# Two attention query projections: three 256-column matmuls per block against one of 512 and one of 256 columns

## The chip, the cores and the metric

One core of one Trainium2 chip runs the whole kernel. The metric is the device time in microseconds (us) of one execution; several executions are timed and their median stands for the kernel.

## The reference

The program is two layers of a decoder trunk on 256 tokens of width 1024, in float32. What matters here, cut down:

```python
for l in range(2):
    h  = layer_norm(ALPHA * x + 0.5 * swiglu(x, w_gu1, w_down1))
    dn_q, dn_k, dn_v, ..., sw_q, sw_k, sw_v, xa_q, gates = split(h @ w_in)
    o_dn = gated_deltanet(dn_q, dn_k, dn_v, ...)              # convolution, SiLU, recurrence
    o_sw = sliding_window_attention(sw_q, sw_k, sw_v, sinks)  # 8 query heads of 64
    o_xa = memory_cross_attention(xa_q, mem_n, w_mem_kv)      # 4 query heads of 128
    h = layer_norm(ALPHA * h + merge(gates, o_dn, o_sw, o_xa) @ w_out)
    x = layer_norm(ALPHA * h + 0.5 * swiglu(h, w_gu2, w_down2))
```

The change is about `xa_q` and `sw_q`, the queries of the two attentions: two products of h (256 x 1024) with a 1024 x 512 part of `w_in`.

## The kernel before

**Split operands.** Every float32 operand of a large product is held as two float32r tiles: hi, the rounded value, and lo, what the rounding left. `split` (lines 115 to 117) makes them: a cast on ACT (line 116), then a subtraction on DVE (line 117). A product is the sum of three: hi by hi, hi by lo, lo by hi.

**Weights.** All weights lie in one stream in the order of their use. `unit` (lines 98 to 113) issues on SP the transfer of the next 1024 columns (512 KB) and splits them into `whi` and `wlo`; there are three raw buffers and five of each split kind. The split of a unit has a raised priority, 300 ahead in the planner's order.

**Activations.** The normalised stream lies transposed in `hT`, 8 blocks of 128 channels by 256 tokens. `new_hT` makes one tile of shape 128 x 8 x 2 x 256, so that a block's hi and lo parts lie side by side: hT[0] is hi, hT[1] is lo, and hT[2][:, k] is both, 512 columns.

**Two ways to project.** `projB_parts` (lines 151 to 165) takes for each block k and each 128-wide output tile t three matmuls of 256 columns, whi by hi, whi by lo and wlo by hi, all into the same half of one PSUM bank; two output tiles share a bank. `halves` (lines 187 to 191) does so for a 512-wide output in two halves of two tiles and gives each finished bank to `use`. `shares` (lines 167 to 185) serves the feed-forward layers: for a block it takes one matmul of 512 columns, whi by hi and lo side by side, into a whole bank of the tile, and one of 256 columns, wlo by hi, into the bank's first half. The sum is then made outside: ACT copies the second half to SBUF (line 183) and DVE adds the first half to it (line 184).

**PSUM.** Matmul results of projections go to the pool `psA`, four banks taken in turn: whoever allocates the fifth waits until the first one's readers are done.

**Order.** Inside `mixers` the flag `pinned` keeps PE's instructions in the order of the program text. For the other engines a planner puts instructions in order by priority, at compile time. `weave(work, steps)` (lines 137 to 141) advances a generator and issues other steps after its n-th part; a half has two parts, one for each unit of weights. The stages of `mixers` around the change are, in order: z, gates of DeltaNet and sw_v (648 columns); the halves of DeltaNet's k, q and v, each followed by `conv`'s `use` (ACT line 486 and six DVE instructions of line 489 per half, which read the bank, then SiLU on ACT, line 490), with the transposes `tok_k` and `tok_q` woven in; then

```python
        weave(halves(xt, use_xq), {3: [tok_v]})
        (b,) = projB(xt, 1, 8)
        ...
        weave(halves(xt, use_sq), {
            1: [decay],
            2: [lambda: spread(0), lambda: x_scores(0)],
            3: [lambda: spread(1)],
            4: [lambda: products(0, 0), lambda: products(0, 1)]})
```

Here `use_xq` and `use_sq` split the finished bank into the hi and lo tiles of the queries (the tiles named u and sql in the profile). `projB(xt, 1, 8)` is sw_k, one unit of weights. `tok_v` transposes the finished v (8 matmuls of line 129) and needs v's last SiLU. `decay` is four small matmuls on g, which DVE makes with a chain of small instructions (lines 550 to 574). After the stage comes `gates(0)`, with matmuls of 512 columns and two banks of `psA` at a time.

Of the kernel before, what the change touches and what calls it, by code (L numbers as in the profile page):

```python
# [17 lines left out]
P = 128  # L18
# [20 lines left out]
def tile_trunk(ctx, tc, x, xT, mem, wst, lnp, memln, cvw, rows, cst, out):  # L39
# [14 lines left out]
    def nm(s):  # L54
        uid[0] += 1
        return f"{s}_{uid[0]}"

    def T(pool, shape, tag, dt=F32, bufs=None):
        kw = {} if bufs is None else {"bufs": bufs}
        return pool.tile(shape, dt, tag=tag, name=nm(tag), **kw)  # L60

    def acc():
        return T(psA, [P, 512], "acc")
# [35 lines left out]
    def unit(w=U, dst=None, cuts=1, behind=None):  # L99
        ahead = tc.high_priority(offset=AHEAD) if pos[0] >= 8 * P * U else nullcontext()  # L100
        raw = T(praw, [P, U], "raw")
        src = wst[pos[0]:pos[0] + P * w].rearrange("(p w) -> p w", p=P)
        pos[0] += P * w
        (ph, th), (pl, tl) = dst or ((phi, "whi"), (plo, "wlo"))
        with ahead:
            hi = T(ph, [P, U], th, F32R)
            lo = T(pl, [P, U], tl, F32R)
            for i in range(cuts):
                c = slice(i * w // cuts, (i + 1) * w // cuts)
                nc.sync.dma_start(raw[:, c], src[:, c])  # L110
                with tc.issue_after(behind) if behind else nullcontext():
                    split(hi[:, c], lo[:, c], raw[:, c])
        return hi, lo

    def split(hi, lo, src):
        nc.scalar.copy(hi, src)  # L116
        return nc.vector.tensor_tensor(lo, src, hi.bitcast(F32), op=ALU.subtract).ins  # L117
# [3 lines left out]
    def pe(ins):  # L121

        return tc.keep_in_program_order(ins) if pinned[0] else ins

    def matmul(*a, **k):
        return pe(nc.tensor.matmul(*a, **k))  # L126
# [10 lines left out]
    def weave(work, steps):  # L137

        for n, _ in enumerate(work, 1):
            for f in steps.get(n, ()):  # L140
                f()

    def projB(xt, nt, kpu, behind=None):
        g = projB_parts(xt, nt, kpu, behind)
        while True:
            try:
                next(g)
            except StopIteration as e:
                return e.value

    def projB_parts(xt, nt, kpu, behind=None):
        banks = [acc().rearrange("p (t s) -> p t s", t=2) for _ in range((nt + 1) // 2)]
        for uu in range(KD // kpu):
            hi, lo = unit(behind=behind)
            for kk in range(kpu):
                k = uu * kpu + kk
                for t in range(nt):
                    c = (kk * nt + t) * P
                    o = banks[t // 2][:, t % 2, :]
                    lastt = t % 2 == 1 or t == nt - 1  # L160
                    matmul(o, hi[:, c:c + P], xt[0](k), start=(k == 0 and t % 2 == 0), stop=False, skip_group_check=True)
                    matmul(o, hi[:, c:c + P], xt[1](k), start=False, stop=False, skip_group_check=True)
                    matmul(o, lo[:, c:c + P], xt[0](k), start=False, stop=(k == KD - 1 and lastt), skip_group_check=True)
            yield
        return banks

    def shares(hT, behind=None):


        banks = [acc() for _ in range(2)]  # L170
        for uu in range(2):
            hi, lo = unit(behind=behind)
            for kk in range(4):
                k = uu * 4 + kk
                cs_ = [slice((kk * 2 + t) * P, (kk * 2 + t + 1) * P) for t in range(2)]

                for t in range(2):
                    matmul(banks[t], hi[:, cs_[t]], hT[2][:, k], start=k == 0, stop=False, skip_group_check=True)
                for t in range(2):
                    matmul(banks[t][:, 0:S], lo[:, cs_[t]], hT[0][:, k, :], start=False, stop=k == KD - 1, skip_group_check=True)  # L180
        y = T(p2, [P, 2, S], "t2", bufs=4)
        for t in range(2):
            nc.scalar.copy(y[:, t], banks[t][:, S:])  # L183
            nc.vector.tensor_tensor(y[:, t], y[:, t], banks[t][:, 0:S], op=ALU.add)  # L184
        return y

    def halves(xt, use):

        for i in range(2):
            (b,) = yield from projB_parts(xt, 2, 4)  # L190
            use(i, b)
# [54 lines left out]
    def new_hT():  # L246

        t = T(pu, [P, KD, 2, S], "hT", F32R)
        return t[:, :, 0, :], t[:, :, 1, :], t

    def acc_of(t):
        return (lambda k: t[0][:, k, :], lambda k: t[1][:, k, :])
# [61 lines left out]
    class Ffn:  # L314
# [54 lines left out]
        def rest(self, hT, tail, dsts, post, mid={}, behind=None):  # L369
            for f in range(2, NFT):  # L370
                y = shares(hT, behind if f == 2 else None)
                nc.scalar.activation(y[:, 0], y[:, 0], AF.Silu)  # L372
                hf = y[:, 1]
                nc.vector.tensor_tensor(hf, y[:, 0], hf, op=ALU.mult)  # L374
                t = self.h(f // 2)
                split(t[:, 0, f % 2, :], t[:, 1, f % 2, :], hf)
                if f in mid:
                    mid[f]()
            outs = full_rows()
            projA((lambda k: self.hu[k // 2][:, 0, k % 2, :], lambda k: self.hu[k // 2][:, 1, k % 2, :]), D, 1, NFT, outs, tail, dsts, after=post)  # L380
# [79 lines left out]
    def mixers(l, hT, mkT, mv_, post):  # L460
        xt = acc_of(hT)
# [79 lines left out]
        def col(tag):  # L541
            return T(pu, sh, tag)
# [11 lines left out]
        t = col("spt")  # L554
        nc.vector.tensor_tensor(t, ba[:, :, 4:8], rowb(rw[:, l, 12:16]), op=ALU.add)
        e = col("spe")
# [16 lines left out]
        g = col("g")  # L573
# [182 lines left out]
        def use_sq(i, b):  # L756
            split(*(t[:, 2 * i:2 * i + 2, :] for t in sq_), b)

        weave(halves(xt, use_xq), {3: [tok_v]})
        (b,) = projB(xt, 1, 8)  # L760
        for kv in range(2):
            hs = slice(kv * 64, kv * 64 + 64)
            split(swk[0][hs, kv, :], swk[1][hs, kv, :], b[hs, 0, :])
        weave(halves(xt, use_sq), {
            1: [decay],
            2: [lambda: spread(0), lambda: x_scores(0)],
            3: [lambda: spread(1)],
# [223 lines left out]
    hT = new_hT()  # L991
# [20 lines left out]
    for l in range(NL):  # L1012
        mT = []
        mid = memory_T(mT, l)
        if l == 0:
            mid.update({5: small, 7: lambda: xres(0), 9: lambda: xres(1)})
        post = Post(lnp[l, 0, 0], lnp[l, 0, 1])
        f1.rest(hT, 4, [((pu, "u12"), (pu, "u13")), ((p2, "gt"), (p2, "gt"))], post, mid, ends)
        kv = memory_kv(mT, post.end)
        if l == 0:  # L1020
            nc.scalar.activation(nea, rw[:, :, 8:12], AF.Exp)
            nc.vector.tensor_scalar(nea, nea, -1.0, None, ALU.mult)
        post2 = Post(lnp[l, 1, 0], lnp[l, 1, 1])
        mixers(l, post.hT, *kv, post2)
        f2 = Ffn()
        begin(f2, post2.hT)
        last = l == NL - 1
        post = Post(lnp[l, 2, 0], lnp[l, 2, 1], last)
        f2.rest(post2.hT, 6, [((pu, a), (pu, b)) for a, b in (("w0", "w1"), ("w2", "w3"), ("u11", "u12"))] + [((pu, "u13"), (p2, "pp"))], post, behind=post2.end)
        ends = post.end  # L1030
        if not last:
            f1, hT = Ffn(), post.hT
            begin(f1, hT)
# [86 lines left out]
```

## Time and profile before

| | |
|---|---|
| time, median of 3 runs | 1296.47 us (1295.87 to 1298.31) |
| the profiled execution's own time | 1298.02 us |
| its span, first to last instruction | 1296.2 us |
| PE / weight loads / DVE / ACT / POOL busy | 99% / 86% / 69% / 55% / 6% |
| granted TensorE clock, mean | 0.998 of full speed |

A line of the timeline reads: start (us from the span's start), how long it was busy, engine, line, operation, tiles written <- tiles read, shape, and how many neighbours were merged; in brackets the idle time of the engine ahead of it and what ended it. Ends of matmuls are modelled, so that two matmuls in a row overlap in the record; from start to start is what one costs.

### The profile page before, as it was taken

Reading aid. Unit: us, or ns where it says so; the run is one execution under the profiler, and the core shown is the slowest. Engines: PE = TensorE matmul, PEld = TensorE weight load, DVE = VectorE, ACT = ScalarE, POOL = GpSimd, SP = SyncE. Lnnn points to the kernel's source line nnn. Section 1 sums busy time; section 2 is a strip of 40 time slices with the busy share of each in tenths; the row PEclk is TensorE's granted clock in tenths of the full one; section 3 lists DMA queues with packets and bytes.
Section 4 is the critical chain, followed back from the end, with each engine's and each line's share of the span. In section 5 each row is a group of like instructions: output and inputs, shape, how many; then the busy total and the mean of one; then the engine's idle time right before and its main releaser. Section 6 shows DMA issues by size and latency. Waiting matters only on the chain.

```text
span 1296.2 us, 20444 instructions
## 1 busy us (share of the span) xinstructions
PE 1277.9 (99%) x7832; PEld 1116.2 (86%) x7832; DVE 888.4 (69%) x1430; ACT 708.5 (55%) x1177; POOL 77.2 (6%) x135
## 2 busy tenths in 40 slices
PE   8999999999999999999999999999999999999997
PEld 6888889999878888888888888899988788888886
DVE  6787556796647777665677674759867388777645
ACT  6656444666674546554455654456656654565541
POOL 0000000102311000000000000000033100000000
PEclk9999999999999999999999999999999999999999
DMA  7867564654533636555665555556453256455553
GB/s 266 276 210 244 193 229 128 220 174 135 161 131 130 228 129 211 191 185 192 228 222 200 188 186 192 199 175 201 163 165 131 98 182 224 149 194 194 189 189 111
DMA packets 68577, 240.25 MB, mean 185 GB/s; under 512 B 8160, under 2 KB 9312, under 8 KB 68480
## 3 DMA queue, kind: packets, MB, share of 16 engines
q1 hardware_dynamic: 66176, 232.53, 53.1%
q0 software_dynamic: 2304, 6.43, 1.8%
q8 instruction: 61, 1.00, 0.3%
q14 instruction: 36, 0.29, 0.1%
HBM read 235.64 MB, written 3.28 MB: 184 GB/s over the span
## 4 chain that ended last, share of the span: by engine, by line
PE 89%; DVE 4%; DMA 4%; ACT 2%; issue 1%; SPq 0%; DVEq 0%; ACTq 0%
PE acc L126 78%; PE at L126 4%; DMA raw<-in_wst_dram 3%; PE sm L126 3%; PE sm L129 1%; ACT whi L116 1%; DVE wlo L117 1%; PE acc L340 1%; PE acc L337 1%; DMA pp<-in_mem_dram 1%; PE acc L338 1%; PE at L129 1%; DVE bnst L282 0%; DVE u L117 0%; DVE h L301 0%
## 5 line engine op out<-in xcount | busy, mean ns | idle before, releaser
L117 DVE TENSOR_TENSOR wlo<-raw,whi 128x1024 fp32r<-128x1024 f32 (+2 forms) x403 | 487.4, 1214 | 308.7 <-ACT whi L116 307.2
L116 ACT CAST whi<-raw 128x1024 fp32r<-128x1024 f32 (+2 forms) x403 | 414.4, 1033 | 366.7 <-DMA raw<-in_wst_dram 99.0
L126 PE MATMUL acc<-hT,whi 128*128 128x512 f32 (+1 forms) x1952 | 524.9, 357 | 0.0
L126 PEld LDWEIGHTS acc<-hT,wlo 128*128 128x128 f32 x1616 | 304.6, 189 | 56.0
L126 PE MATMUL acc<-hT,wlo 128*128 128x256 f32 x1616 | 347.6, 279 | 0.0
L126 PEld LDWEIGHTS acc<-hT,whi 128*128 128x128 f32 x1952 | 299.8, 190 | 0.2
L126 PE MATMUL acc<-whi,u 128*128 128x512 f32 (+1 forms) x800 | 246.7, 373 | 0.0
L126 PEld LDWEIGHTS acc<-whi,u 128*128 128x128 f32 x800 | 150.1, 188 | 27.7 <-DVE t L184 1.2
L126 PE MATMUL acc<-whi,hT 128*128 128x512 f32 (+1 forms) x544 | 168.4, 380 | 5.6 <-ACT whi L116 5.6
L126 PE MATMUL acc<-wlo,u 128*128 128x512 f32 (+1 forms) x400 | 148.4, 371 | 0.0
L126 PEld LDWEIGHTS acc<-whi,hT 128*128 128x128 f32 x544 | 100.6, 189 | 23.7 <-ACT whi L116 5.6
L126 PE MATMUL acc<-wlo,hT 128*128 128x512 f32 (+1 forms) x272 | 101.9, 375 | 0.0
L126 PEld LDWEIGHTS acc<-wlo,u 128*128 128x128 f32 x400 | 75.5, 189 | 12.2
L372 ACT ACTIVATE t<-t 128x256 f32<-128x256 f32 x80 | 33.4, 417 | 60.4 <-DVE t L184 59.9
L184 DVE TENSOR_TENSOR t<-t,acc 128x256 f32<-128x256 f32 x160 | 59.9, 415 | 0.0
L126 PEld LDWEIGHTS acc<-wlo,hT 128*128 128x128 f32 x272 | 51.5, 190 | 8.2 <-DVE wlo L117 0.9
L183 ACT COPY t<-acc 128x256 f32<-128x256 f32 x160 | 51.5, 369 | 0.1
L116 ACT CAST u<-t 128x256 fp32r<-128x256 f32 x80 | 32.1, 401 | 20.4 <-DVE t L374 20.4
L374 DVE TENSOR_TENSOR t<-t 128x256 f32<-128x256 f32 x80 | 33.9, 424 | 9.2 <-ACT t L372 7.7
L126 PE MATMUL at<-whi,u 128*128 128x256 f32 x152 | 39.0, 283 | 0.0
L117 DVE TENSOR_TENSOR u<-t,u 128x256 fp32r<-128x256 f32 x80 | 33.6, 420 | 7.1 <-ACT u L116 7.1
L489 DVE SCALAR_TENSOR_TENSOR t<-acc,cw,t 128x255 f32<-128x255 f32 (+2 forms) x72 | 34.5, 479 | 0.9
(248 smaller groups left out, 1250.4 us busy)
## 6 DMA issues: line engine op xcount, KB each, us to landing
raw<-in_wst_dram SPq DMA_DIRECT2D x409, 512.0 KB, 3.6
raw<-in_wst_dram SPq DMA_DIRECT2D x16, 324.0 KB, 3.0
gB<-in_lnp_dram SPq DMA_DIRECT2D x6, 512.0 KB, 6.4
bB<-in_lnp_dram SPq DMA_DIRECT2D x6, 512.0 KB, 5.9
mdr<-w POOLq DMA_DIRECT2D x4, 512.0 KB, 6.8
w<-dr POOLq DMA_DIRECT2D x4, 512.0 KB, 8.8
w<-mdr POOLq DMA_DIRECT2D x4, 512.0 KB, 5.2
t<-in_xT_dram SPq DMA_DIRECT2D x4, 256.0 KB, 5.3
```

Of the source, the lines that this page charges most:

```text
L116: nc.scalar.copy(hi, src)
L117: return nc.vector.tensor_tensor(lo, src, hi.bitcast(F32), op=ALU.subtract).ins
L126: return pe(nc.tensor.matmul(*a, **k))
L129: return pe(nc.tensor.transpose(*a))
L183: nc.scalar.copy(y[:, t], banks[t][:, S:])
L184: nc.vector.tensor_tensor(y[:, t], y[:, t], banks[t][:, 0:S], op=ALU.add)
L337: nc.tensor.matmul(ps, hT[0][:, k, ts], hi[:, c], start=k == 0, stop=False)
L338: nc.tensor.matmul(ps, hT[0][:, k, ts], lo[:, c], start=False, stop=False)
L340: nc.tensor.matmul(ps, hT[1][:, k, ts], hi[:, c], start=False, stop=k == KD - 1)
L372: nc.scalar.activation(y[:, 0], y[:, 0], AF.Silu)
L374: nc.vector.tensor_tensor(hf, y[:, 0], hf, op=ALU.mult)
L489: nc.vector.scalar_tensor_tensor(yc[:, j, d:], b[:, j, :S - d], w[:, t:t + 1], yc[:, j, d:], op0=ALU.mult, op1=ALU.add)
```

## The change

`shares` becomes a generator, `shares_parts`, that yields after each unit of weights and can be woven; the old `shares` runs it to its end, so the feed-forward layers issue what they issued. A new `wide_halves` runs it twice for a 512-wide output, and the queries of both attentions use it in place of `halves`. The split of the queries (`use_xq`, `use_sq`) then reads a sum in SBUF and not a bank.

```diff
     def shares(hT, behind=None):
-
-
-        banks = [acc() for _ in range(2)]
-        for uu in range(2):
+        g = shares_parts(hT, behind)
+        while True:
+            try:
+                next(g)
+            except StopIteration as e:
+                return e.value
+
+    def shares_parts(hT, behind=None, nt=2):
+        kpu = 8 // nt
+        banks = [acc() for _ in range(nt)]
+        for uu in range(nt):
             hi, lo = unit(behind=behind)
-            for kk in range(4):
+            for kk in range(kpu):
...
-                for t in range(2):
+                for t in range(nt):
                     matmul(banks[t], hi[:, cs_[t]], hT[2][:, k], start=k == 0, stop=False, skip_group_check=True)
-                for t in range(2):
+                for t in range(nt):
                     matmul(banks[t][:, 0:S], lo[:, cs_[t]], hT[0][:, k, :], start=False, stop=k == KD - 1, skip_group_check=True)
+            yield
         y = T(p2, [P, 2, S], "t2", bufs=4)
-        for t in range(2):
+        for t in range(nt):
             nc.scalar.copy(y[:, t], banks[t][:, S:])
             nc.vector.tensor_tensor(y[:, t], y[:, t], banks[t][:, 0:S], op=ALU.add)
         return y
+
+    def wide_halves(hT, use):
+
+        for i in range(2):
+            use(i, (yield from shares_parts(hT)))
...
-        weave(halves(xt, use_xq), {3: [tok_v]})
+        weave(wide_halves(hT, use_xq), {3: [tok_v]})
...
-        weave(halves(xt, use_sq), {
+        weave(wide_halves(hT, use_sq), {
```

## Rows read from the trace of the kernel before

**Rows 1.** The page: busy time of the engines, slices, the chain that ended last.

```profile
PE 1277.9 (99%) x7832; PEld 1116.2 (86%) x7832; DVE 888.4 (69%) x1430; ACT 708.5 (55%) x1177; POOL 77.2 (6%) x135
...
PE 89%; DVE 4%; DMA 4%; ACT 2%; issue 1%; SPq 0%; DVEq 0%; ACTq 0%
```

**Rows 2.** By stretch: length, PE, PEld, DVE, ACT, POOL busy, clock, DMA share, GB/s.

```profile
235.00:271.00 36.00, 36.00 (x304) 36.00 (x303) 32.63 (x63) 22.92 (x35) 2.38 (x2) 1.00 0.58 200
271.00:284.00 13.00, 13.00 (x111) 13.00 (x110) 11.69 (x25) 8.25 (x13) 0.00 (x0) 1.00 0.47 160
284.00:304.00 20.00, 20.00 (x170) 19.92 (x169) 14.22 (x32) 12.76 (x26) 3.12 (x2) 1.00 0.47 159
```

**Rows 3.** Timeline of PE, first layer: first half of xa_q, second half's first row.

```profile
271.26 0.40 PE L126 MATMUL acc<-hT,whi 128*128 128x256 f32 x2
271.50 0.28 PE L126 MATMUL acc<-hT,wlo 128*128 128x256 f32 x1
...
277.02 0.40 PE L126 MATMUL acc<-hT,whi 128*128 128x256 f32 x2
```

**Rows 4.** Timeline of PE, feed-forward layer: two passes of the other scheme.

```profile
63.87 0.62 PE L126 MATMUL acc<-hT,whi 128*128 128x512 f32 x2
64.33 0.40 PE L126 MATMUL acc<-hT,wlo 128*128 128x256 f32 x2
...
75.02 0.63 PE L126 MATMUL acc<-hT,whi 128*128 128x512 f32 x2
```

**Rows 5.** Groups by line: weight load, copy and add of the other scheme, split.

```profile
L126 PEld LDWEIGHTS acc<-hT,whi 128*128 128x128 f32 x1952 | 299.8, 190 | 0.2
...
L184 DVE TENSOR_TENSOR t<-t,acc 128x256 f32<-128x256 f32 x160 | 59.9, 415 | 0.0
L183 ACT COPY t<-acc 128x256 f32<-128x256 f32 x160 | 51.5, 369 | 0.1
```

**Rows 6.** Timeline of DVE, first layer: end of v's convolution, split of xa_q.

```profile
276.45 1.51 DVE L489 SCALAR_TENSOR_TENSOR t<-acc,cw,t 128x255 f32<-128x255 f32 x3
278.18 1.23 DVE L117 TENSOR_TENSOR wlo<-raw,whi 128x1024 fp32r<-128x1024 f32 x1 [0.22 <-ACT whi L116]
```

**Rows 7.** Timeline of ACT, first layer: around the end of xa_q's first half.

```profile
274.22 1.05 ACT L116 CAST whi<-raw 128x1024 fp32r<-128x1024 f32 x1 [0.94 <-PE acc L126]
275.17 0.47 ACT L486 ACTIVATE t<-acc,cw 128x256 f32<-128x256 f32 x1
277.10 1.05 ACT L116 CAST whi<-raw 128x1024 fp32r<-128x1024 f32 x1 [1.46 <-PE acc L126]
```

**Rows 8.** From a DVE result to PE's start: timelines of DVE and PE.

```profile
459.63 1.41 DVE L301 SCALAR_TENSOR_TENSOR h<-h,rstd,bB 128x512 f32<-128x512 f32 x2
...
460.53 0.63 PE L129 MATMUL sm<-cs,h 128*128 128x128 f32 x4 [0.97 <-DVE h L301]
```

**Rows 9.** The same place in the second layer: PE, then DVE.

```profile
916.92 0.40 PE L126 MATMUL acc<-hT,whi 128*128 128x256 f32 x2
...
916.35 1.51 DVE L489 SCALAR_TENSOR_TENSOR t<-acc,cw,t 128x255 f32<-128x255 f32 x3
```

**Rows 10.** First layer, PE: tok_v, sw_k's start, sw_q's start.

```profile
279.90 1.04 PE L129 MATMUL sm<-cs,u 128*128 128x128 f32 x8
280.69 0.48 PE L126 MATMUL acc<-hT,whi 128*128 128x256 f32 x2
...
286.52 0.40 PE L126 MATMUL acc<-hT,whi 128*128 128x256 f32 x2
```

**Rows 11.** First layer, ACT then DVE: split of xa_q's second half and its neighbours.

```profile
283.72 1.05 ACT L116 CAST whi<-raw 128x1024 fp32r<-128x1024 f32 x1 [1.98 <-PE acc L126]
...
285.01 1.23 DVE L117 TENSOR_TENSOR wlo<-raw,whi 128x1024 fp32r<-128x1024 f32 x1
...
286.23 0.69 DVE L117 TENSOR_TENSOR u<-acc,u 128x512 fp32r<-128x512 f32 x1
...
287.44 0.17 DVE L574 TENSOR_TENSOR g<-spp,nea 128x8 f32<-128x8 f32 x1
```

More of the change, by code (lines that the diff above doesn't have):

```diff
@@ L167, in shares @@
     def shares(hT, behind=None):
-        banks = [acc() for _ in range(2)]
-        for uu in range(2):
+        g = shares_parts(hT, behind)
[8 more added lines that the diff above has]
+        for uu in range(nt):
             hi, lo = unit(behind=behind)
-            for kk in range(4):
-                k = uu * 4 + kk
-                cs_ = [slice((kk * 2 + t) * P, (kk * 2 + t + 1) * P) for t in range(2)]
-                for t in range(2):
+            for kk in range(kpu):
+                k = uu * kpu + kk
+                cs_ = [slice((kk * nt + t) * P, (kk * nt + t + 1) * P) for t in range(nt)]
+                for t in range(nt):
                     matmul(banks[t], hi[:, cs_[t]], hT[2][:, k], start=k == 0, stop=False, skip_group_check=True)
-                for t in range(2):
+                for t in range(nt):
                     matmul(banks[t][:, 0:S], lo[:, cs_[t]], hT[0][:, k, :], start=False, stop=k == KD - 1, skip_group_check=True)
+            yield
         y = T(p2, [P, 2, S], "t2", bufs=4)
-        for t in range(2):
+        for t in range(nt):
             nc.scalar.copy(y[:, t], banks[t][:, S:])
```

## The prediction

> **What bounds the kernel now.** I read the page first: PE is busy 99% of the span and 89% of the chain that ended last is PE's [rows 1]. So what a change is worth must appear as time of PE, and of PE in the stage that is changed. The stretches of the first layer say the same of that stage: between 235 and 304 us PE and the weight loads are busy all the time at the full clock (1.00, the 2.4 GHz level), while DVE has 32.63 of 36.00 us before the queries, 11.69 of 13.00 us during xa_q and 14.22 of 20.00 us behind it [rows 2]. PE is the bound; DVE is the engine with least to spare. A busy PE is no measure of what a matmul costs, since the modelled ends overlap, so I take distances from start to start in the timeline, and for what may wait I read DVE and ACT around the ends of the halves.
>
> **PE's saving.** A half has 8 blocks by 2 tiles, 16 products of three matmuls. Its first starts at 271.26 us and the next half's first at 277.02 us: 5.76 us, or 0.36 us for a product, 0.12 for each 256-column matmul [rows 3]. In the feed-forward layers `shares` does a product of the same size with two matmuls; from 63.87 to 75.02 us two such passes of 16 products follow each other, 11.15 us, so 5.575 us each [rows 4]. The columns are the same, 768 in both; what goes is one matmul and one weight load in three, and what that is worth is 5.76 - 5.575 = 0.185 us a half. Two halves, two attentions, two layers make 8 halves: 1.48 us, 0.11% of the time. Nothing in the trace suggests that `shares` would run at another distance here: same tiles, same clock.
>
> The Trainium skill (TensorE: Matmul & The Clock Gate, Back-to-back issue gap) puts the isolated matmul of N columns at N / 2.4 + 2.5 ns; by it the product would fall from 327.5 to 325.0 ns, and 128 products would give an estimated 0.3 us. The measured distance of 0.12 us, not its 109 ns, decides here.
>
> **What is added.** Each half now needs two ACT copies of 0.369 us and two DVE adds of 0.415 us [rows 5] ahead of the split that was there: in all 16 copies, 5.9 us of ACT, and 16 adds, 6.6 us of DVE. I cost their busy time at nothing: per layer DVE gets 3.3 us more, and it has 1.3 us idle during xa_q and 5.8 us behind it [rows 2]. Where that cover is gone, the weights' splits come later; but ACT's casts of weights wait for PE to free a buffer (0.94 and 1.46 us, [rows 7]), so the five buffers are full, and a delay of DVE of 1 or 2 us does not reach PE by that way. The transfers, SP's queue and POOL get nothing new and nothing is moved past them; the woven steps stand behind the same units.
>
> **What is held longer: banks.** A half took one bank of `psA` and now takes two, one per tile. Counting the allocations in the order of the text: v's two halves take banks 0 and 1, xa_q's first half 2 and 3, its second half 0 and 1 again, sw_k bank 2, sw_q's halves 3 and 0, then 1 and 2, and `gates(0)` starts with the pair 3 and 0. So xa_q's second half, whose second matmul goes to bank 1, must wait until the convolution of v's second half has read that bank. That convolution ends on DVE at 276.45 + 1.51 = 277.96 us [rows 6]. It is late since ACT's multiplication ahead of it (line 486, at 275.17) stands behind a weight cast that waits for PE [rows 7]. With the change this cast is released 0.09 us earlier (half the saving of a half), so I take 277.87. PE is there at 271.26 + 5.575 + 0.23 = 277.07, the 0.23 being what the 512-column matmul ahead costs (0.46 from 63.87 to 64.33 for two, [rows 4]). From a DVE result to PE's start I take 0.15 us: the first of two instructions of line 301 ends at about 460.35 and PE starts at 460.53 [rows 8]. The wait: 277.87 + 0.15 - 277.07 = 0.95 us. In the second layer the half starts at 916.92 and the convolution ends at 917.86, the same 0.94 apart as 277.02 and 277.96 [rows 9, 3, 6], so 0.95 again. Behind the waiting matmul, in order, are the rest of that half, `tok_v`, sw_k and sw_q; ACT's next weight cast waits for them too.
>
> The bank is bounded from below by zero (if the planner puts the convolution earlier) and from above by what a whole further weight split ahead of it on DVE would add, 1.23 us [rows 6], so 2.2 us. I take 0.95, since the row is of this very convolution.
>
> Next candidate: sw_q's first half, whose second matmul needs bank 0 of xa_q's second half. PE's shift there is -0.37 + 0.95, so it comes to 286.52 + 0.58 + 0.23 = 287.33 [rows 10]. ACT's cast at 283.72 shifts with PE to 284.3 and ends at 285.35; the copy follows to 285.7; DVE's weight split (285.01 before, [rows 11]) runs from 285.6 to 286.8, the add from there to 287.2, plus 0.15 of passing on: 287.35. Nothing to 0.1 us; I take 0.02. The upper bound is in the second rival. `tok_v` (279.90) shifts with PE, and the pair of `gates(0)` was filled 17 us earlier.
>
> **Sum:** -1.48 + 2 x (0.95 + 0.02) = +0.46 us. The profiled execution took 1298.02 us (span 1296.2 and 1.8 around it), so 1298.5 of that; the median of the runs, 1296.47, lies 1.55 us lower, and against it I forecast 1296.9 us. A measurement of this kernel can tell about 0.2% from no change, 2.6 us, so 1293.9 and 1299.1 are the borders: no change that can be seen. With the bank's wait between 0 and 2.2 us a layer the forecast's own range is 1295.0 to 1299.5.
>
> **Rivals.**
> *No wait: only the saving.* If the planner, which now knows that PE waits for the bank, brings ACT's line 486 ahead of the weight cast, bank 1 is free in time: 1296.47 - 1.48 = 1295.0 us. For it: ACT is idle for 0.94 us right ahead of that cast [rows 7]. Against: weights keep their raised priority.
>
> *Slower: the add of xa_q's second half is put behind the chain for g.* The split of that half stood in the middle of DVE's chain, 1.2 us ahead of g's last instruction [rows 11]. What is to be split is now ready later by a copy and an add; if the chain goes first and delayed by DVE's extra work, the add starts after g, at 287.6 + 0.8 (xa_q's first adds) = 288.4, and ends at 288.8; PE, due at 287.33, gets bank 0 at 288.95 and waits 1.6 us, 3.2 in both layers: 1296.9 + 3.2 = 1300.1 us. It decides as soon as that add starts after about 286.8. For it: DVE is at 90% during xa_q [rows 2]. Against: the chain's small instructions leave gaps, and bank 0 is awaited by PE.
>
> *Much faster: the loads are the bound.* Weight loads are busy 100% of the stage [rows 2] at 190 ns each [rows 5]. Were that their cost, 128 loads less would give 128 x 0.190 = 24 us: 1272.2 us. Against it, decisively: matmuls with a load each follow every 0.12 us [rows 3], so loads overlap. The Trainium skill (Perfetto Trace Analysis, Identifying the Most-Contended Engine) calls the busy share of the weight loads a good measure of TensorE's headroom, which would favour this rival; here that share is 100% and still counts overlapping loads.
>
> **How the numbers follow.** The forecast 0.50, no wait 0.22, the add behind the chain 0.22, the loads 0.02; 0.04 for an order of DVE or ACT that changes elsewhere, either way. Faster by over 0.2% needs the loads, or 1.1 us besides the whole saving: 0.02 + 0.07 + 0.02 = 0.11. Slower: most of the add's case, 0.18, a tail of the forecast, 0.04, and half of the rest, 0.02: 0.24. The remaining 0.65 is no change. The range takes in no wait with 1 us of chance below, and the add with 1 us above: 1294.0 to 1301.1 us.
>
> **What would show it.** Right: 7704 matmuls for 7832; halves of the queries 5.58 us long but for one wait of about 1 us at the second matmul of xa_q's second half, just after line 489 ends, in both layers. Wrong: no such wait (first rival), a wait at sw_q's first half with the add after g (second), or a half much under 5.5 us (third). A stage shorter by over 2 us, or PE waiting at `tok_v` or for weights, would mean that I missed a mechanism.

## The result and the profile after

The changed kernel took 1299.96 us against 1297.76 us before (medians of 12 runs each). The ratio is 1.0017, with a 95% interval of 1.0009 to 1.0024: 2.2 us slower. That is inside the prediction's range and inside the 0.2% that it called no change, but the interval lies clear of 1, so the loss is real, and it is 1.7 us more than the +0.46 us forecast. (The 1296.47 us that the prediction started from was the median of 3 of these 12 runs.)

The page of the profile after (span 1298.3 us, 2.1 us more than before):

```profile
PE 1278.1 (98%) x7704; PEld 1109.2 (85%) x7704; DVE 892.4 (69%) x1446; ACT 713.3 (55%) x1193; POOL 76.8 (6%) x135
...
q8 instruction: 60, 0.98, 0.3%
```

128 matmuls and loads less, 16 instructions more on DVE and on ACT, as counted. The second line is of the DMA queues: the queue that carries instructions moved 60 packets of 16 KB, one less than before (61, 1.00 MB). It looked like nothing and turned out to be half of the story.

The stage itself, on PE's timeline of the first layer after the change, from the last blocks of xa_q's first half into the second:

```profile
276.20 0.62 PE L126 MATMUL acc<-hT,whi 128*128 128x512 f32 x2
276.67 0.40 PE L126 MATMUL acc<-hT,wlo 128*128 128x256 f32 x2
276.90 0.39 PE L126 MATMUL acc<-hT,whi 128*128 128x512 f32 x1
277.97 0.47 PE L126 MATMUL acc<-hT,whi 128*128 128x512 f32 x1 [0.68 <-ACT whi L116]
278.27 0.40 PE L126 MATMUL acc<-hT,wlo 128*128 128x256 f32 x2
```

and on DVE's at the same place (line 504 is line 489 of before):

```profile
275.17 1.23 DVE L117 TENSOR_TENSOR wlo<-raw,whi 128x1024 fp32r<-128x1024 f32 x1
276.31 1.51 DVE L504 SCALAR_TENSOR_TENSOR t<-acc,cw,t 128x255 f32<-128x255 f32 x3
```

The first half ran from 271.32 to 276.90 us, 5.58 us for 5.76 before [rows 3]. The second half's first matmul starts at 276.90 us, its second not 0.23 but 1.07 us later, 0.15 us after the convolution has ended (276.31 + 1.51 = 277.82): a wait of 0.84 us. The second layer shows the same, 918.00 to 919.07 us. The bracket names an ACT cast, which merely ended at about the same moment (the first matmul of that half already reads `whi` of the same unit); the run with another bank below shows that it was the bank. Sw_q's halves have no wait. From `tok_k` to the first matmul of `products` the first layer's stage took 46.77 us (255.19 to 301.96) for 46.55 before, the second layer's 46.77 (896.29 to 943.06) for 46.55: +0.44 us for both.

So the stage gave nearly what was forecast, and the rest of the 2.1 us lies elsewhere. Walking along PE's timeline with both kernels side by side, the distance stays at +0.27 us for 136 us, up to w_out, the product behind the merge. There the first layer shows, before the change:

```profile
438.08 0.40 PE L126 MATMUL acc<-wlo,w 128*128 128x512 f32 x1
438.80 0.50 PE L126 MATMUL acc<-whi,w 128*128 128x512 f32 x1 [0.33 <-DVE w L117]
```

and after it:

```profile
438.03 0.48 PE L126 MATMUL acc<-whi,w 128*128 128x512 f32 x1
438.35 0.40 PE L126 MATMUL acc<-wlo,w 128*128 128x512 f32 x1
440.19 0.50 PE L126 MATMUL acc<-whi,w 128*128 128x512 f32 x1 [1.45 <-DVE w L117]
```

From 438.35 to 440.19 is 1.85 us; the kernel before took 0.72 there, and in the second layer 1.56 stands against 0.73. (These distances from start to start are called the wait at w_out from here on.) PE waits for DVE, DVE stands in line behind splits of w_out's weights, and ACT's casts of these wait for transfers. ACT after the change:

```profile
429.79 1.05 ACT L116 CAST u<-raw 128x1024 fp32r<-128x1024 f32 x1 [1.76 <-DMA raw<-in_wst_dram]
432.52 1.05 ACT L116 CAST u<-raw 128x1024 fp32r<-128x1024 f32 x1 [1.69 <-DMA raw<-in_wst_dram]
435.80 1.05 ACT L116 CAST u<-raw 128x1024 fp32r<-128x1024 f32 x1 [2.22 <-DMA raw<-in_wst_dram]
```

and before:

```profile
428.60 1.05 ACT L116 CAST u<-raw 128x1024 fp32r<-128x1024 f32 x1 [0.84 <-DMA raw<-in_wst_dram]
431.29 1.05 ACT L116 CAST u<-raw 128x1024 fp32r<-128x1024 f32 x1 [1.64 <-DMA raw<-in_wst_dram]
434.09 1.05 ACT L116 CAST u<-raw 128x1024 fp32r<-128x1024 f32 x1 [1.75 <-DMA raw<-in_wst_dram]
```

The three start 1.2, 1.2 and 1.7 us later, 0.27 of which is the stage's. Nothing in the code differs here, ACT's and DVE's instructions follow one another in the same order in both traces from 314 to 917 us, and yet the weights come later. Some of it is given back: the transposes behind the next LayerNorm wait 0.39 us less. Of the 2.1 us between the two spans 0.44 are the stage's, 1.13 the first w_out's and 0.83 the second's; the rest of the program gives back 0.3.

### The profile page after: what moved, and what is told of

The parts are those of the page before. It is cut to its first block, busy times and chain, and to the rows that moved or that the text cites. A ratio compares the mean times of both kernels' runs of the same rounds, so it can differ in the third digit from the quotient of the medians.

```text
span 1298.3 us, 20216 instructions
## 1 busy us (share of the span) xinstructions
PE 1278.1 (98%) x7704; PEld 1109.2 (85%) x7704; DVE 892.4 (69%) x1446; ACT 713.3 (55%) x1193; POOL 76.8 (6%) x135
## 4 chain that ended last, share of the span: by engine, by line
PE 87%; DMA 4%; DVE 4%; ACT 3%; issue 1%; SPq 0%; DVEq 0%; ACTq 0%
PE acc L126 76%; PE at L126 5%; DMA raw<-in_wst_dram 4%; PE sm L126 3%; ACT whi L116 2%; PE sm L129 1%; DVE wlo L117 1%; PE acc L355 1%; PE acc L352 1%; DVE h L315 1%; PE at L129 1%; PE acc L353 0%; DVE bnst L297 0%; DVE h L316 0%; DVE u L117 0%
## 5 line engine op out<-in xcount | busy, mean ns | idle before, releaser
L126 PE MATMUL acc<-hT,whi 128*128 128x512 f32 (+1 forms) x1824 | 519.3, 371 | 1.7 <-ACT whi L116 1.4
L126 PE MATMUL acc<-hT,wlo 128*128 128x256 f32 x1616 | 336.3, 279 | 0.0
L126 PEld LDWEIGHTS acc<-hT,whi 128*128 128x128 f32 x1824 | 279.6, 189 | 2.9 <-ACT whi L116 1.9
L194 DVE TENSOR_TENSOR t<-t,acc 128x256 f32<-128x256 f32 x176 | 66.3, 415 | 0.0
L193 ACT COPY t<-acc 128x256 f32<-128x256 f32 x176 | 56.9, 370 | 0.0
L116 ACT CAST u<-t 128x256 fp32r<-128x256 f32 (+1 forms) x88 | 37.0, 421 | 20.8 <-DVE t L389 20.7
L117 DVE TENSOR_TENSOR u<-t,u 128x256 fp32r<-128x256 f32 (+1 forms) x84 | 38.0, 453 | 7.1 <-ACT u L116 7.1
```

## The experiments

The question is what lengthened w_out: that one execution's transfers, the stage's new order, or something that the change moved there; the theories and their numbers stand in the expectations. Kernels measured together ran on one chip, each beside the kernel before.

**Both kernels again, unchanged.** Is the wait at w_out the change's, or that execution's? (`rep_before`, `rep_after`: no edit.)

> The kernel before, unchanged, timed and profiled once more. Theory 1 (stage): the change costs only its balance in the stage, 8 x 0.185 us saved against a wait of 0.83 us for a bank in each layer, +0.2 us a layer; the wait ahead of w_out (0.72 us from start to start in the old profile of before, 1.85 and 1.56 us in that of after) differs since the transfers of that execution took longer on average, and will here come out anywhere between 0.7 and 1.9 us. Theory 2 (downstream): the change itself makes the weights of w_out late, so here the two w_out waits are again 0.7 us. Ratio to before 1.000 within 0.001 by both.

> The changed kernel, unchanged, on the same chip as the run above. Theory 1: bank waits of 0.83 us again in both layers, w_out waits like those of the repeated before within 0.3 us, span longer than the repeated before's by 0.4 to 0.8 us, ratio 1.0003 to 1.0010. Theory 2: w_out waits 1.5 to 1.9 us against 0.7, span longer by about 2 us, ratio 1.0015 to 1.0020.

Measured: ratio 0.9996 (0.9987 to 1.0005) and 1.0018 (1.0010 to 1.0027). The repeated before, at w_out:

```profile
438.87 0.40 PE L126 MATMUL acc<-wlo,w 128*128 128x512 f32 x1
439.59 0.50 PE L126 MATMUL acc<-whi,w 128*128 128x512 f32 x1 [0.33 <-DVE w L117]
```

The repeated after:

```profile
440.78 0.40 PE L126 MATMUL acc<-wlo,w 128*128 128x512 f32 x1
442.69 0.50 PE L126 MATMUL acc<-whi,w 128*128 128x512 f32 x1 [1.52 <-DVE w L117]
```

0.73 and 1.91 us: the first layer's wait belongs to the changed kernel, and theory 1 in its plain form, that it was one execution's transfers, falls. The second layer's did not come back (0.73 in both); that one was the single execution's, and its cause was not found: the transfers of the same weights were late there too, though the last packet of the kind described below started 20 us ahead.

**One part alone.** Only sw_q in the new way:

```diff
-        weave(wide_halves(hT, use_xq), {3: [tok_v]})
+        weave(halves(xt, use_xq), {3: [tok_v]})
```

> Only sw_q uses the new matmuls, xa_q the old ones. Theory 1: no bank wait of its second half, since four allocations back lies the first half of xa_q, long read; the saving of 4 halves stays, 0.74 us: products end 0.37 us earlier in each layer, ratio 0.9994. Theory 2: w_out still waits 1.5 us or more in each layer, ratio 1.0005 to 1.0010.

Measured: ratio 0.9996 (0.9987 to 1.0005); from `tok_k` to `products` 46.20 us in the first layer (255.43 to 301.63), 0.35 less than before for two halves, against 2 x 0.185 = 0.37 forecast; no bank wait; w_out waits 0.73 us in both layers. The saving is real, and the bank wait comes with xa_q alone. The longer wait at w_out is gone too, which speaks against theory 2 as far as it blames sw_q; what it hangs on comes out below. The ratio itself is too small to be told from 1.

**The bank taken away.** xa_q's second half gets its second bank from the attentions' pool:

```diff
-        banks = [acc() for _ in range(nt)]
+        banks = [at() if spare and t else acc() for t in range(nt)]
```

> The change, with the second tile of xa_q's second half in a bank of the attention pool that nobody uses at that time. Theory 1: the bank wait is gone, so the stage is 0.74 us shorter than before in each layer, 1.48 us in all, ratio 0.9989 (1295.0 us by the median of the prediction). If the wait moves instead to tok_v or to sw_q's first half, the gain is less than 0.5 us a layer. Theory 2: gain eaten by waits at w_out, ratio 1.000 or above.

Measured: ratio 1.0018 (1.0009 to 1.0027). The bank wait is gone, which shows that it was the bank: the second matmul starts 0.23 us after the first, while the convolution (275.82 + 1.51 = 277.33) and the ACT cast still run. But PE now waits at `decay`: its start is 1.14 us behind that of the matmuls ahead, where the changed kernel takes 0.24 (289.70 to 289.94), so 0.90 us; in the second layer 0.89. PE of this run:

```profile
276.41 0.40 PE L126 MATMUL acc<-hT,whi 128*128 128x512 f32 x1
276.64 0.40 PE L126 MATMUL at<-hT,whi 128*128 128x512 f32 x1
...
288.29 0.40 PE L126 MATMUL acc<-hT,wlo 128*128 128x256 f32 x2
289.43 0.58 PE L126 MATMUL sm<-g,cs 128*128 128x8 f32 x4 [0.74 <-DVE g L589]
```

and DVE:

```profile
286.91 1.23 DVE L117 TENSOR_TENSOR wlo<-raw,whi 128x1024 fp32r<-128x1024 f32 x1
...
288.12 0.68 DVE L117 TENSOR_TENSOR u<-t,u 128x512 fp32r<-128x512 f32 x1
...
288.80 0.41 DVE L117 TENSOR_TENSOR swk<-acc,swk 64x256 fp32r<-64x256 f32 x1
289.13 0.15 DVE L589 TENSOR_TENSOR g<-spp,nea 128x8 f32<-128x8 f32 x1
```

In the changed kernel g comes ahead of those three splits:

```profile
287.59 0.17 DVE L589 TENSOR_TENSOR g<-spp,nea 128x8 f32<-128x8 f32 x1
288.32 1.64 DVE L117 TENSOR_TENSOR wlo<-raw,whi 128x1024 fp32r<-128x1024 f32 x1 [0.56 <-ACT whi L116]
289.88 1.52 DVE L117 TENSOR_TENSOR u<-t,u 128x512 fp32r<-128x512 f32 x1
291.33 0.41 DVE L117 TENSOR_TENSOR swk<-acc,swk 64x256 fp32r<-64x256 f32 x1
```

From `tok_k` to `products` it is 46.84 us (254.70 to 301.54): no shorter than the changed kernel. The stall had not covered for g: in the changed kernel g is ready at 287.76 us, 2.2 us ahead of `decay` and so by more than the whole bank wait. With the spare bank the planner put some 2.3 us of splits ahead of it (1.23 + 0.68 + 0.41), and it comes at 289.28. The first w_out waits 2.04 us.

**Decay later.** The spare bank, and `decay` behind the second unit of sw_q:

```diff
-            1: [decay],
-            2: [lambda: spread(0), lambda: x_scores(0)],
+            2: [decay, lambda: spread(0), lambda: x_scores(0)],
```

> The change with the spare bank, and decay woven in behind the second unit of sw_q and not the first. Theory 1 in its second form (the bank wait once gone, PE waits 1.03 us at decay for g, whose chain DVE's adds and PE's lead make late): with decay 2.8 us later no wait is left, and from the start of xa_q to the start of products is 0.74 us shorter than before in each layer. The w_out wait of the first layer stays at about 2 us if the instruction packet is where it was (theory 3). Ratio about 0.9998. Rival (DVE is the bound of the stage): PE waits again, at spread, for what POOL makes of g, and the stage is no shorter than in the changed kernel.

Measured: from `tok_k` to `products` 45.93 us (254.79 to 300.72) and 45.85 (895.12 to 940.97), 0.62 and 0.70 less than before, where 0.74 was expected: no wait is left in the stage, and DVE, in nearly the same order as in the run before, is not its bound. The first w_out waits 1.99 us, as expected by theory 3, and the ratio is 1.0006 (0.9997 to 1.0014), for 0.9998 expected.

**What reaches the weights at w_out: 64 small matmuls.** A list of the instruction queue's packets beside PE's instructions shows one of 16 KB for about every 256 instructions of PE, loads and matmuls, 0.9 us and more long, where a packet of weights has 4 KB. One starts 13.6, 13.5 and 14.4 us ahead of the first layer's w_out in the profiles of after, of its repeat and of the spare bank; in the two of before the nearest lie 26.8 us ahead and 6.7 or 8.5 behind, with sw_q alone 20.9 ahead. The distances fit the counts: up to the first w_out the change takes out 64 matmuls and 64 loads, half of 256, and the packet lies 13 us nearer; sw_q alone takes out a quarter, and it lies 6 us nearer. To move them, these kernels run small matmuls on zeros ahead of everything:

```diff
+    idle = pc.tile([P, 32], F32, name="idle")
+    nc.vector.memset(idle, 0.0)
+    ps = sm()
+    for _ in range(64):
+        matmul(ps[0:32, 0:32], idle[0:32, :], idle[0:32, :], start=True, stop=True)
     hT = new_hT()
```

> The kernel before, with 64 matmuls of 32 columns on a tile of zeros put ahead of everything while PE waits for the first weights: 128 more instructions of PE (loads and matmuls), nothing else. In all runs so far a packet of 16 KB on the queue for instructions comes about once in 256 instructions of PE; in the kernels whose xa_q uses the new matmuls one starts 13 to 14 us ahead of the first layer's w_out, in the others none lies within 20 us ahead of it. Theory 3 (instruction fetch): the place of that packet decides, so here, moved by half a period, it starts about 14 us ahead of w_out, and the first layer's wait at w_out grows from 0.73 to 1.7 to 2.1 us though nothing of the change is in the kernel. Rival (the change delays the weights by DVE's or ACT's order): the wait stays 0.73 us. The start itself may gain or lose up to 1 us.

> The changed kernel with the same 128 instructions of PE ahead of it. Theory 3: the instruction packet moves out of the 20 us ahead of the first layer's w_out and the wait there falls from 1.9 to about 0.73 us, with the bank wait of 0.83 us as it was; about 1.1 us less than the changed kernel, apart from what the start does. Rival: the wait stays 1.9 us.

> The kernel above with the 128 instructions of PE ahead of it. If theories 1 and 3 both hold: no wait in the stage, 0.73 us at the first layer's w_out; 1.48 us less than before, ratio 0.9985 to 0.9992 apart from the start. If either falls: 0.9995 or above.

Measured: ratios 1.0006 (0.9998 to 1.0015), 1.0021 (1.0011 to 1.0030) and 1.0009 (1.0000 to 1.0017). The packets had not moved: 26.9, 13.4 and 14.7 us ahead. The page of the padded before tells why:

```profile
PE 1284.4 (99%) x7960; PEld 1123.4 (87%) x7960; DVE 885.8 (68%) x1431; ACT 708.4 (55%) x1177; POOL 78.3 (6%) x135
...
q8 instruction: 62, 1.02, 0.3%
```

128 matmuls and 128 loads more for 64 written: each of these float32 matmuls is two. That is 256 instructions, one whole packet more or one period, and a whole period moves nothing. The expectations' premise fell, not the theory: with the packet where it was, the wait at the first w_out was 0.73 us in the padded before and 1.10 and 1.70 in the other two. The 7 us of small matmuls also put PE's first real matmul off to 7.98 us, from about 5.

**Half as many.** 32 small matmuls, 128 instructions, with each of the three kernels:

> As the padded kernel before, with 32 small matmuls and not 64: each of these float32 matmuls came out as two loads and two matmuls, so 64 were 256 instructions, one whole period, and moved nothing. 32 are 128, half a period. Theory 3 (instruction fetch): a packet of the instruction queue now starts 12 to 16 us ahead of the first layer's w_out, and the wait there is 1.1 to 2.1 us in a kernel that has nothing of the change. Rival (the planner's order of DVE and ACT, not the packet): 0.73 us.

> The changed kernel with the same 128 instructions ahead. Theory 3: packets about 26 us ahead of and 7 us behind the first layer's w_out, as in the kernel before, and the wait there 0.73 us; both bank waits 0.83 us as they were; span about 1.1 us shorter than the changed kernel's, ratio about 1.0008. Rival: 1.1 to 1.9 us.

> The change with the spare bank, decay one unit later and the 128 instructions ahead. If theories 1 and 3 hold: no wait in the stage, 0.73 us at both w_outs, 1.3 to 1.5 us less than before, ratio 0.9985 to 0.9995. If the packet is not the cause, the first w_out waits 1.7 to 2.0 us and the ratio is 0.9998 to 1.0008.

The kernel before with half a period ahead of it, PE at the first w_out:

```profile
437.64 0.39 PE L126 MATMUL acc<-wlo,w 128*128 128x512 f32 x1
439.25 0.73 PE L126 MATMUL acc<-whi,w 128*128 128x512 f32 x2 [1.23 <-DVE w L117]
```

and its DMA queues in the 16 us ahead of that (packets, MB, share of 16 engines; then issues, KB each, median us to landing):

```profile
q1 hardware_dynamic: 864, 3.15, 63.1%
q8 instruction: 1, 0.02, 0.4%
...
raw<-in_wst_dram SPq DMA_DIRECT2D x6, 512.0 KB, 3.8
```

The changed kernel with half a period ahead of it, PE:

```profile
440.39 0.39 PE L126 MATMUL acc<-wlo,w 128*128 128x512 f32 x1
441.12 0.50 PE L126 MATMUL acc<-whi,w 128*128 128x512 f32 x1 [0.34 <-DVE w L117]
```

and its queues in the 16 us ahead:

```profile
q1 hardware_dynamic: 815, 2.95, 53.4%
q14 instruction: 1, 0.01, 0.1%
...
raw<-in_wst_dram SPq DMA_DIRECT2D x6, 512.0 KB, 3.3
```

(The 16 KB packets are those of queue q8; q14 is another, with packets of 8 KB.) For the three transfers alone that the casts above wait for, the kernel before with 64 small matmuls ahead (424.6 to 430.2 us), then with 32 (422.4 to 428.0 us):

```profile
raw<-in_wst_dram SPq DMA_DIRECT2D x3, 512.0 KB, 3.2
```

```profile
q8 instruction: 1, 0.02, 1.1%
...
raw<-in_wst_dram SPq DMA_DIRECT2D x3, 512.0 KB, 4.2
```

The two have changed places. The kernel before, with nothing of the change, now has a packet 13.4 us ahead and waits 1.62 us; the changed one has its packets 26.8 us ahead and 3.5 behind, and waits 0.73. Its bank waits are as they were (1.07 us from start to start). Ratios: 1.0003 (0.9993 to 1.0012) and 0.9998 (0.9989 to 1.0007), where about 1.0008 was expected of the second. In all 13 profiles the first w_out waits 1.10 to 2.04 us in the seven with a packet 13.4 to 14.7 us ahead of it, and 0.72 or 0.73 us in the six others, on at least two chips. In the seven the packet starts while the first of the three transfers is under way, and the median of the three from issue to landing is 3.8 to 4.3 us, against 3.2 or 3.3 in the six. The rival, an order of DVE or ACT, is out: with 64 and with 32 small matmuls ahead, the kernel before has the same order on both from 41 us on.

With the spare bank, the later `decay` and the 128 instructions together the kernel took 1295.72 us against 1297.69, ratio 0.9985 (0.9976 to 0.9994): faster than both. Its first w_out waits 0.73 us, and from `tok_k` to `products` it takes 45.84 us (255.62 to 301.46). Two expectations were missed: the gain is 2.0 us, where 1.3 to 1.5 were expected, and the second w_out waits 1.06 us and not 0.73. There a packet starts 9.5 us ahead, just after the third transfer was issued, which takes 3.9 us to land.

## Why the prediction was right, and where it fell short

**PE's saving: right.** 0.185 us a half was forecast; xa_q's first half fell from 5.76 to 5.58 us [rows 3], and with sw_q alone the stage is 0.35 us shorter for two halves. The distance that the feed-forward layers showed [rows 4] carried over unchanged.

**The bank: right, slightly too large.** The wait is where it was put, at the second matmul of xa_q's second half in both layers, 0.84 us for 0.95. The convolution ended at 277.82 for the 277.87 taken, and PE was at 277.13 for 277.07; 0.15 us from DVE's end to PE's start [rows 8] was measured again here. With it the stage adds up: where no wait is left it is 0.71 us shorter a layer (46.55 to 45.84), and the matmul that waited takes 0.07 us more than the usual 0.23 (277.97 to 278.27), so 0.84 + 0.07 - 0.71 = 0.20 a layer for the 0.22 measured. A second wait at sw_q's first half was put at 0.02 us, and none is there.

**Costs put at nothing: right here, not by the reason given alone.** DVE's adds did not reach PE in the changed kernel. Idle time of DVE [rows 2] was named as the cover, but what decides is the order that the planner makes: with the spare bank and the same adds, other splits went ahead of g, and it was 0.9 us late. The second rival had this chain in it, with the add behind g and PE waiting for bank 0; it came true in neither kernel, and the chain delays PE by g itself.

**The sum: +0.46 forecast, +2.2 (1.2 to 3.1) measured.** The stage gave +0.44. The step that failed is "The transfers, SP's queue and POOL get nothing new and nothing is moved past them": a change that takes out PE instructions also moves the transfers that bring instructions, and one of them came to lie where w_out's weights are late anyway. That wait grew by 1.1 to 1.2 us in both profiles of the changed kernel. This, less what LayerNorm gives back, and the stage make some 1.2 to 1.6 us, inside the measured interval. PE waiting for weights stood among the prediction's own signs of a missed mechanism. That 1299.96 us lies in the range all the same is partly luck: the room above 1299.5 was left for the second rival, which did not come true. Against the 1297.76 us of these runs the +2.2 us would also fit a bank wait of some 1.8 us a layer, which the range allowed for; the bank took 0.84. The first rival's 1295.0 us would not have come from the bank alone either: it took three edits to get there.

**Not settled:** the ratio moves by more between the changed kernel and its half-padded twin (1.0018 to 0.9998) than the wait at w_out does (1.2 us, 0.0009). The spare bank with the later decay shows the same: 1.0006 to 0.9985, 2.7 us for a wait 1.3 us shorter. The intervals just allow it, and the work ahead of the stage alone differs by 2.2 us between the seven profiles without small matmuls (the first matmul that reads a tile named w starts at 195.3 to 197.5 us), but what else the packets' places change was not measured. Nor was it shown why transfers stay late for three units, or how a packet of 0.9 us does it; in the second layer of the changed kernel's first profile they were as late (4.2 us) without one.

## What to carry to other kernels

Count banks along with matmuls: a scheme that holds two for one makes PE wait for the readers of the allocation four back, and if that wait is removed, look again at the order that the planner makes: here it put 2.3 us of splits ahead of a result that PE needed next. When the trace shows a delay far from the edit, at an unchanged order, look at what shares the DMA engines there, the instruction queue's packets too: a kernel's number of PE instructions sets their places, so a change of 0.1% can be outweighed by where they fall, and shifting them by half a period with dummy instructions tells the two apart. Count the instructions as the profile records them, since one that is written can be two.

## What the runs showed of the hardware

One packet of 16 KB on the instruction queue for about 256 PE instructions (61, 60 and 62 packets for 15664, 15408 and 15920 loads and matmuls), each some 0.9 us long at least, where 4 KB of weights have a median of 0.16 us. One of them 13 to 15 us ahead of the first w_out, a place that is short of weights, went with 3.8 to 4.3 us from issue to landing (median of three transfers of 512 KB, seven profiles), where 3.2 or 3.3 stand without one (six profiles). Elsewhere it mostly costs less: of the 427 transfers, 147 have a packet that starts within 3 us after their issue in at least two of the 13 profiles and none in at least two others, and the median difference of the landing is 0.26 us. A small float32 matmul, on tiles that are not float32r, is recorded as two loads and two matmuls.
